# Two decoder layers on one core: the latent keys' token factors spread over the partitions by two transfers through DRAM

## The chip, the cores and the metric

The kernel runs on one core of a Trainium2 chip. The metric is the device time of one execution in microseconds (us); before the change its median over three runs is 1880.4 us (1880.3 to 1882.12). PE is the matrix engine, DVE the vector engine, ACT the scalar engine, POOL the GpSimd engine, and SP issues most of the loads. Each engine works through its own list of instructions in the order in which the list was written at build time, and waits where an instruction needs something that another engine or a transfer has not finished.

## The reference, cut to what matters

Two layers of a decoder trunk over 512 tokens and 1024 channels. In each layer a branch of multi-head latent attention makes keys and values from a normalised low-rank vector `c_kv` of 256 channels per token:

```
kv = (rmsnorm(c_kv, norm_kv) @ w_ukv).reshape(bsz, seq, MLA_HEADS, QK_NOPE + V_DIM)
k_nope, v = kv[..., :QK_NOPE], kv[..., QK_NOPE:]
```

with `rmsnorm(x, g) = x * rsqrt(mean(x*x) + EPS) * g`. The factor `rsqrt(...)` is one number per token. Four heads have 128 key and 128 value channels each. Around this branch stand the combined input projection, a convolution branch, sparse attention, a merge of the branches, cross attention and a SwiGLU block.

## The kernel before

Products are made three times over with high and low parts of each operand (lines 86 to 88: high by high, high by low, low by high), and `hilo` (lines 93 and 94, or 96 and 97 with a scale) makes these parts: ACT writes the high part, DVE the low part. Weights come by SP into `raw`, become `wh` and `wl`, and are used once.

The token factors of the latent attention are made in `mix`, once in each layer. PE sums the squares of the latents per token into one bank (`means`, line 1210), so that the tokens lie on the partitions: column t holds tokens 128 t to 128 t + 127. DVE adds the epsilon (line 1213) and POOL takes the power -1/2 (line 1214). Of the tile `rst`, columns 0 to 3 then hold the four query factors and columns 4 to 7 the four key factors. The latents are kept without their factor, and it is put in later:

- `values` has the tokens on the partitions, so the factor is a scale per partition (`rst[:, 4 + t]`, lines 96 and 97).
- `keys(h)` has the key channels on the partitions and the 512 tokens along the row, so it needs the factors as a row of 512 numbers, the same on all 128 partitions. This is the tile `rk`; line 846 multiplies the product in PSUM by it (`kf`), and `hilo` splits the result.

`scales` makes `rk`. DVE multiplies the identity by each of the four columns (line 820, tile `dg`, four diagonal blocks of 128), PE multiplies a tile of ones by `dg` (line 833), which puts each token's factor on every partition, and ACT copies the bank to `rk` (line 835). `scales` also splits the weights of keys and values (`weights`).

The code of `mix` runs several strands in turn: `pump` hands out steps of `filler`, which are the input projection's products for the sparse attention, so that PE has work between the dependent steps of the latent attention. A scheduler then puts every engine's instructions in an order at build time. The banks of PSUM are few: tags `mm` (3), `pv` (1), `s` (2) and `t` (2). `idle` hands out `s`, `t`, `s`, `t`, `pv` in turn for queries, keys, `turned` (transposes of the rotated queries, drained at lines 409 and 410) and values. A product on PE waits until DVE and ACT have read the bank that it takes over.

POOL issues background transfers of its own: sums of weight blocks from DRAM to DRAM (`up`, `down`, `mixed`, line 481) which a much later stage reads. Each of them waits for a certain product on PE (`tick`), and POOL stands still until then. The powers and a few small fills stand in the same list.

Of the kernel before, what the change touches and what calls it, by code (L numbers as in the profile page):

```python
# [10 lines left out]
F32 = mybir.dt.float32  # L11
# [3 lines left out]
OP = mybir.AluOpType  # L15
# [6 lines left out]
NT = T // 128  # L22
# [30 lines left out]
def kernel(ctx, tc, x, mem, positions, rel_bias, norm_mix, norm_xattn, norm_mem, norm_ffn, norm_final,  # L53
# [5 lines left out]
    nc = tc.nc  # L59
# [6 lines left out]
    dr = ctx.enter_context(tc.tile_pool(name="dr", bufs=1, space=DRAM))  # L66
# [7 lines left out]
    def new(tag, shape=(128, 512), dt=F32, name=None):  # L74
        return (odd if tag in ODD else sb).tile(list(shape), dt, name=name or tag, tag=tag, bufs=BUFS[tag])

    def bank(tag, name=None):
        return ps.tile([128, 512], F32, name=name or f"ps_{tag}", tag=tag, bufs=PBUFS[tag])
# [11 lines left out]
    def hilo(hi, lo, src, scale=None):  # L90

        if scale is None:
            nc.scalar.copy(hi, src)  # L93
            nc.vector.tensor_tensor(lo, src, f(hi), op=OP.subtract)  # L94
        else:
            nc.scalar.activation(hi, src, AF.Copy, scale=scale)
            nc.vector.scalar_tensor_tensor(lo, src, scale, f(hi), op0=OP.mult, op1=OP.subtract)
# [68 lines left out]
    ident = cst.tile([128, 128], F32, name="ident")  # L166
    ones = cst.tile([128, 128], F32, name="ones")
# [318 lines left out]
    def mix(l, x_src, g_mix, x_now, more_x, spill_x, turns, memory):  # L486
# [136 lines left out]
        for i, wu in enumerate(fm_blocks(W, [Z_CQ, Z_CQ + 128, Z_CQ + 256, Z_CKV, Z_CKV + 128], KD)):  # L623
            p = bank("mm")
# [190 lines left out]

        def scales():
            nc.vector.tensor_scalar(rst[:, 8:12], rst[:, 0:4], -(128 + 64) ** -0.5, None, op0=OP.mult)
            dg = new("P", name="dg")
            for t in range(NT):
                nc.vector.tensor_scalar(dg[:, t * 128:(t + 1) * 128], ident, rst[:, 4 + t:5 + t], None, op0=OP.mult)  # L820
            rv = kv_raw.rearrange("p (k h c) -> p k h c", k=2, h=4)

            def weights(c0):
                w = new("wh", (128, 1024), F32R), new("wl", (128, 1024), F32R)
                for k in range(2):
                    hilo(w[0][:, k * 512:(k + 1) * 512].rearrange("p (h c) -> p h c", h=4),
                         w[1][:, k * 512:(k + 1) * 512].rearrange("p (h c) -> p h c", h=4), rv[:, k, :, c0:c0 + 128])
                wk.append(w)

            weights(0)  # L830
            yield
            p = bank(next(idle))
            nc.tensor.matmul(p, ones, dg, start=True, stop=True)
            rk = new("gm", name="rk")
            nc.scalar.copy(rk, p)
            weights(128)
            yield rk

# [362 lines left out]
        idle = cycle(("s", "t", "s", "t", "pv"))  # L1201
# [6 lines left out]
        for i, q in enumerate(sq):  # L1208
            for t in range(NT):
                nc.tensor.matmul(means[:, i * 4 + t:i * 4 + t + 1], q[:, t * 128:(t + 1) * 128], ones[:, 0:1],  # L1210
                                 start=True, stop=True)
        rst = new("rst", (128, 16))
        nc.vector.tensor_scalar(rst[:, 8:16], means[:, 0:8], EPS, None, op0=OP.add)
        nc.gpsimd.tensor_tensor(rst[:, 0:8], rst[:, 8:16], mhalf, op=OP.pow)

        scale = scales()
        qrot = []
        for t in range(NT):
            p = bank(next(idle))
# [8 lines left out]
            rk = next(scale) if t % 2 else None  # L1228
# [263 lines left out]
    for l in range(L):  # L1492
# [75 lines left out]
        for h, wu in enumerate(fm_blocks(w_xkv[l], [128 * h for h in range(4)], KD)):  # L1568
            p = bank("mm")
# [177 lines left out]
        for i, wu in enumerate(fm_blocks(w_gate_up[l], cols, KD)):  # L1747
            m = i % 2
            p = bank("mm")
# [189 lines left out]
```

## Time and profile before

| | |
|---|---|
| median of three runs | 1880.4 us |
| profiled execution, its own time | 1880.6 us |
| span of the profiled execution | 1878.9 us |
| clock granted to PE | 0.999 of full |
| DVE busy | 1554.9 us (83%) |
| ACT busy | 1067.9 us (57%) |
| POOL busy | 317.8 us (17%) |

The profiled execution lies within the three runs. The two places that make `rk` lie at about 85 to 89 us (first layer) and 1016 to 1019 us (second layer) from the start of the span. In the rows of the timeline the first number is the start, the second how long the instruction or the run of instructions took; the bracket at a row's end gives the idle time of that engine just ahead of it and what ended it.

### The profile page before, as it was taken

What the parts mean: (1) busy time and instruction counts of PE and PEld (TensorE: products, weight loads), DVE (VectorE), ACT (ScalarE), POOL (GpSimd) and SP (SyncE); (2) the same over time, 40 slices, a digit from 0 to 9 for tenths busy, and PEclk for the clock granted to TensorE, in tenths of its full rate; (3) what the DMA queues carried; (4) which work ended last, traced back from release to release, by engine and by line L of the source; (5) the groups of instructions that cost most, each with busy time, mean ns of one, the idle gap of its engine ahead of it and who ended that gap; (6) DMA issues with size and microseconds to landing.
All of it is one profiled execution on the core that took longest, in us unless ns stands there. A gap on an engine that the chain in (4) does not pass through costs nothing.

```text
span 1878.9 us, 29709 instructions
## 1 busy us (share of the span) xinstructions
PE 1863.0 (99%) x10940; PEld 1634.2 (87%) x10940; DVE 1554.9 (83%) x2842; ACT 1067.9 (57%) x1992; POOL 317.8 (17%) x501
## 2 busy tenths in 40 slices
PE   9999999999999999999999999999999999999998
PEld 8888888888887999998888888888888889999986
DVE  6999998765966899898869999986659678899886
ACT  5367557764555545456544755686636455445564
POOL 1211112112121212200022111121121122212000
PEclk9999999999999999999999999999999999999999
DMA  6665765568774778876666666655786747877764
GB/s 188 160 164 158 186 151 142 132 165 201 230 213 129 197 193 219 224 218 200 180 188 166 167 176 169 150 120 137 172 212 206 222 139 194 215 192 215 229 191 162
DMA packets 229901, 341.60 MB, mean 182 GB/s; under 512 B 17600, under 2 KB 157139, under 8 KB 229756
## 3 DMA queue, kind: packets, MB, share of 16 engines
q1 hardware_dynamic: 188460, 222.68, 37.4%
q0 software_dynamic: 39360, 112.22, 28.5%
q10 hardware_dynamic: 1936, 4.81, 0.7%
q8 instruction: 86, 1.41, 0.3%
q14 instruction: 59, 0.48, 0.1%
HBM read 330.20 MB, written 114.32 MB: 237 GB/s over the span
## 4 chain that ended last, share of the span: by engine, by line
PE 86%; DVE 5%; issue 5%; POOL 1%; ACT 1%; DMA 1%; SPq 0%; POOLq 0%; DVEq 0%; ACTq 0%
PE ps_mm L86 15%; PE ps_mm L88 14%; PE ps_mm L87 14%; PE ps_s L86 3%; PE ps_s L88 2%; PE ps_s L87 2%; PE ps_t L88 2%; PE ps_t L87 2%; PE ps_t L86 2%; PE ps_t L1130 2%; PE ps_mm L1440 1%; PE ps_mm L1441 1%; PE ps_mm L1439 1%; PE ps_pv L86 1%; PE ps_s L1439 1%
## 5 line engine op out<-in xcount | busy, mean ns | idle before, releaser
L93 ACT CAST wh<-raw 128x1024 fp32r<-128x1024 f32 (+4 forms) x429 | 434.9, 1016 | 473.6 <-PE ps_mm L87 110.8
L94 DVE TENSOR_TENSOR wl<-raw,wh 128x1024 fp32r<-128x1024 f32 (+4 forms) x429 | 503.1, 1177 | 173.3 <-ACT wh L93 169.6
L86 PE MATMUL ps_mm<-hTh,wh 128*128 128x512 f32 (+1 forms) x1152 | 415.1, 361 | 0.0
L87 PE MATMUL ps_mm<-hTl,wh 128*128 128x512 f32 (+1 forms) x1152 | 411.2, 357 | 0.0
L88 PE MATMUL ps_mm<-hTh,wl 128*128 128x512 f32 (+1 forms) x1152 | 410.5, 357 | 0.5 <-DVE wl L94 0.5
L88 PEld LDWEIGHTS ps_mm<-hTh,wl 128*128 128x128 f32 x1152 | 217.8, 189 | 32.8 <-DVE wl L94 1.3
L86 PEld LDWEIGHTS ps_mm<-hTh,wh 128*128 128x128 f32 x1152 | 217.9, 189 | 28.4 <-issue 1.3
L87 PEld LDWEIGHTS ps_mm<-hTl,wh 128*128 128x128 f32 x1152 | 218.0, 189 | 26.2 <-issue 0.7
L602 DVE SCALAR_TENSOR_TENSOR ca<-u,vT,ca 128x512 f32<-128x512 f32 x240 | 177.7, 747 | 2.8
L481 POOL DMA_DIRECT2D up<-in_w_gate_up_dram x128 | 84.7, 662 | 459.8 <-PE ps_mm L88 343.8
L481 POOL DMA_DIRECT2D down<-in_w_down_dram x132 | 87.8, 674 | 287.3 <-PE ps_mm L88 134.4
L93 ACT CAST PTh<-ps_t 128x512 fp32r<-128x512 f32 (+4 forms) x136 | 70.2, 516 | 50.6 <-PE ps_t L1130 43.8
L1093 ACT ACTIVATE P<-P,ss 128x512 f32<-128x512 f32 (+3 forms) x128 | 71.5, 559 | 48.2 <-DVE ss L1090 47.2
L86 PE MATMUL ps_s<-rh,wh 128*128 128x256 f32 x320 | 90.6, 283 | 0.0
L87 PE MATMUL ps_s<-rl,wh 128*128 128x256 f32 x320 | 90.6, 283 | 0.0
L88 PE MATMUL ps_s<-rh,wl 128*128 128x256 f32 x320 | 90.6, 283 | 0.0
L94 DVE TENSOR_TENSOR PTl<-ps_t,PTh 128x512 fp32r<-128x512 f32 (+2 forms) x120 | 71.7, 599 | 10.2 <-ACT PTh L93 9.1
L1101 ACT ACTIVATE P<-P,sr 128x512 f32<-128x512 f32 (+3 forms) x128 | 63.2, 555 | 13.7 <-DVE sr L1099 13.6
L481 POOL DMA_DIRECT2D down<-down x44 | 35.5, 807 | 189.4 <-DMA down<-down 79.1
L200 POOL TENSOR_TENSOR rs<-rs,mhalf 128x1 f32<-128x1 f32 x25 | 24.1, 964 | 229.9 <-DVE rs L197 229.8
L86 PEld LDWEIGHTS ps_s<-rh,wh 128*128 128x128 f32 x320 | 61.4, 192 | 0.0
L87 PEld LDWEIGHTS ps_s<-rl,wh 128*128 128x128 f32 x320 | 61.4, 192 | 0.0
(598 smaller groups left out, 4803.8 us busy)
## 6 DMA issues: line engine op xcount, KB each, us to landing
up<-in_w_gate_up_dram POOLq DMA_DIRECT2D x128, 320.0 KB, 4.4
down<-in_w_down_dram POOLq DMA_DIRECT2D x132, 256.0 KB, 5.1
raw<-in_w_in_dram SPq DMA_DIRECT2D x30, 1024.0 KB
raw<-in_w_gate_up_dram SPq DMA_DIRECT2D x60, 512.0 KB
raw<-up SPq DMA_DIRECT2D x40, 512.0 KB
raw<-down SPq DMA_DIRECT2D x40, 512.0 KB
raw<-in_w_in_dram SPq DMA_DIRECT2D x30, 512.0 KB
raw<-in_w_down_dram SPq DMA_DIRECT2D x30, 512.0 KB
```

What stands on the lines that cost most here:

```text
L86: nc.tensor.matmul(o, lh, rh, start=start, stop=False)
L87: nc.tensor.matmul(o, lh, rl, start=False, stop=False)
L88: tick(nc.tensor.matmul(o, ll, rh, start=False, stop=stop))
L93: nc.scalar.copy(hi, src)
L94: nc.vector.tensor_tensor(lo, src, f(hi), op=OP.subtract)
L200: latest["power"] = nc.gpsimd.tensor_tensor(r[:, 1:2], r[:, 0:1], mhalf[:, 0:1], op=OP.pow)
L481: d = nc.gpsimd.dma_start(dst, src, accum_op=op) if op else nc.gpsimd.dma_start(dst, src)
L602: nc.vector.scalar_tensor_tensor(c, u[:, j:j + T], cw[:, m, j:j + 1], c, op0=OP.mult, op1=OP.add)
L1093: nc.scalar.activation(p[:, c], p[:, c], AF.Exp, bias=s[:, k:k + 1], scale=-1.0, accum_out=s[:, 4 + k:5 + k])
L1101: nc.scalar.activation(P[k], P[k], AF.Copy, scale=r[:, k:k + 1])
L1130: nc.tensor.transpose(tp[:, w:w + 128], P[k][:, j * 128:(j + 1) * 128], ident)
L1439: nc.tensor.matmul(accs[t], xh, u[0][:, k, :], start=j == 0 and not goes_on, stop=False, **kw)
```

## The change

The diagonal tile, the product with ones and the copy out of PSUM go. In their place stand two transfers that POOL issues: one writes columns 4 to 7 of `rst`, 128 x 4 numbers, into a small DRAM tile `spread` in the order of the tokens, and one reads these 512 numbers back to all 128 partitions of `rk`. The call that took a bank from `idle` stays without the bank, so the turns of the banks don't shift.

```diff
         def scales():
             nc.vector.tensor_scalar(rst[:, 8:12], rst[:, 0:4], -(128 + 64) ** -0.5, None, op0=OP.mult)
-            dg = new("P", name="dg")
-            for t in range(NT):
-                nc.vector.tensor_scalar(dg[:, t * 128:(t + 1) * 128], ident, rst[:, 4 + t:5 + t], None, op0=OP.mult)
+            spread = dr.tile([NT, 128], F32, name=f"spread{l}")
+            rk = new("gm", name="rk")
+            nc.gpsimd.dma_start(spread.rearrange("t p -> p t"), rst[:, 4:8])
+            nc.gpsimd.dma_start(rk, bass.AP(tensor=spread.tensor, offset=spread.offset, ap=[[0, 128], [1, 512]]))
             rv = kv_raw.rearrange("p (k h c) -> p k h c", k=2, h=4)
...
             weights(0)
             yield
-            p = bank(next(idle))
-            nc.tensor.matmul(p, ones, dg, start=True, stop=True)
-            rk = new("gm", name="rk")
-            nc.scalar.copy(rk, p)
+            next(idle)
             weights(128)
             yield rk
```

The lines of the new kernel are one higher from 821 to 831 and two lower from 834 on (846 becomes 844).

The scheduler writes some instructions near the place in another order. Three places follow. The first is POOL's list in the first layer, from the power (line 1214 before, 1212 now) on. Before:

```order
L1214 TENSOR_TENSOR rst<-rst,mhalf 128x8
L481 DMA up_2_149<-in_w_gate_up_dram 64x1280
L481 DMA up_0_148<-in_w_gate_up_dram 64x1280
L481 DMA up_2_149<-in_w_gate_up_dram 64x1280
L481 DMA up_0_148<-in_w_gate_up_dram 64x1280
L593 MEMSET u 128x30
```

Now:

```order
L1212 TENSOR_TENSOR rst<-rst,mhalf 128x8
L820 DMA spread_956<-rst 128x4x1
L481 DMA up_2_149<-in_w_gate_up_dram 64x1280
L821 DMA rk<-spread_956 128x512
L481 DMA up_0_148<-in_w_gate_up_dram 64x1280
L481 DMA up_2_149<-in_w_gate_up_dram 64x1280
L481 DMA up_0_148<-in_w_gate_up_dram 64x1280
L593 MEMSET u 128x30
```

The write stands right behind the power, one background sum behind it, and then the read, which waits for the write to have landed. The second layer has the same order.

The second place is DVE's list in the second layer, from the split of the second head's `kf` to the product of the third head with `rk` (`xf` and `xt` are inputs of the sparse attention's compression, `wl` the low part of weights that PE waits for). Before:

```order
L94 TENSOR_TENSOR op_10923<-kf_10924,op_10922 128x512
L664 TENSOR_TENSOR xf_10945<-ps_mm_10791,vT_10175 64x496
L410 SCALAR_TENSOR_TENSOR op_10933<-ps_t_10928,op_10933 64x512
L94 TENSOR_TENSOR xt_10942<-xf_10945,xt_10942 128x8x31 x2
L664 TENSOR_TENSOR xf_10945<-ps_mm_10791,vT_10175 64x496
L410 SCALAR_TENSOR_TENSOR op_10936<-ps_t_10928,op_10936 64x512
L664 TENSOR_TENSOR xf_10945<-ps_mm_10791,vT_10175 64x496
L94 TENSOR_TENSOR wl_10962<-raw_10958,wh_10961 128x1024
L94 TENSOR_TENSOR xt_10942<-xf_10945,xt_10942 128x8x31 x2
L846 TENSOR_TENSOR kf_10979<-ps_pv_10969,rk_10866 128x512
```

Now:

```order
L94 TENSOR_TENSOR op_10913<-kf_10914,op_10912 128x512
L410 SCALAR_TENSOR_TENSOR op_10923<-ps_t_10918,op_10923 64x512
L94 TENSOR_TENSOR xt_10932<-xf_10935,xt_10932 128x8x31 x2
L664 TENSOR_TENSOR xf_10935<-ps_mm_10786,vT_10170 64x496 x2
L410 SCALAR_TENSOR_TENSOR op_10926<-ps_t_10918,op_10926 64x512
L94 TENSOR_TENSOR xt_10932<-xf_10935,xt_10932 128x8x31 x2
L94 TENSOR_TENSOR wl_10952<-raw_10948,wh_10951 128x1024
L844 TENSOR_TENSOR kf_10969<-ps_pv_10959,rk_10811 128x512
```

One `xf` moved ahead of the first of these rows, and the last pair of `xt` moved from behind `wl` to ahead of it. In the first layer it is the other way round: there a pair of `xt` moved from ahead of `wl` to behind it. On PE, two products of `values` that stood behind the product with this `wl` now stand ahead of it in the second layer; in the first layer one product of the input projection moved from ahead of it to behind it.

The third place is ACT's list in the second layer, from the split of the fourth head's `kf` to the first softmax of the latent attention (`P`; the scale of the finished row is line 888 before, 886 now). Before:

```order
L93 CAST op_10996<-kf_10998 128x512
L93 CAST wh_11198<-raw_10792 128x1024
L96 ACTIVATE op_11010<-ps_t_11002,rst_10771 128x512
L96 ACTIVATE op_11021<-ps_s_11014,rst_10771 128x512
L886 ACT_TABLE_LOAD
L886 ACTIVATE P_11054,s1_11055<-P_11054,s1_11055 128x512
L96 ACTIVATE op_11032<-ps_t_11025,rst_10771 128x512
L93 CAST w1_11208<-raw_11210 128x512
L96 ACTIVATE op_11044<-ps_pv_11036,rst_10771 128x512
L888 ACTIVATE P_11054<-P_11054,s1_11055 128x512
```

Now:

```order
L93 CAST op_10986<-kf_10988 128x512
L93 CAST wh_11188<-raw_10787 128x1024
L96 ACTIVATE op_11000<-ps_t_10992,rst_10766 128x512
L96 ACTIVATE op_11011<-ps_s_11004,rst_10766 128x512
L96 ACTIVATE op_11022<-ps_t_11015,rst_10766 128x512
L96 ACTIVATE op_11034<-ps_pv_11026,rst_10766 128x512
L93 CAST w1_11198<-raw_11200 128x512
L93 CAST w1_11199<-raw_11200 128x512
L93 CAST wh_11306<-raw_11303 128x1024
L884 ACT_TABLE_LOAD
L884 ACTIVATE P_11044,s1_11045<-P_11044,s1_11045 128x512
```

Two splits of `values`, two of `w1` and the split of the next weights `wh` moved ahead of the table load and the first exponential.

## The prediction

> **What bounds the kernel now.** I read the page's busy times and its chain first, then the two stretches where `rk` is made. Each row is busy time and share of the span; the second is the chain that ended last.
>
> ```profile
> PE 1863.0 (99%) x10940; PEld 1634.2 (87%) x10940; DVE 1554.9 (83%) x2842; ACT 1067.9 (57%) x1992; POOL 317.8 (17%) x501
> PE 86%; DVE 5%; issue 5%; POOL 1%; ACT 1%; DMA 1%; SPq 0%; POOLq 0%; DVEq 0%; ACTq 0%
> ```
>
> PE is hardly ever idle. So work taken from PE is worth its length, a wait that PE takes on costs its length, and work off PE counts only where PE waits for it. The timeline of PE has one such wait in each of the two stretches, and both are for DVE:
>
> ```profile
> 102.56 0.47 PE L86 MATMUL ps_t<-wh,op 128*128 128x512 f32 x1 [0.25 <-DVE op L410]
> 104.38 0.50 PE L88 MATMUL ps_mm<-hTh,wl 128*128 128x512 f32 x1
> 1033.72 0.50 PE L88 MATMUL ps_mm<-hTh,wl 128*128 128x512 f32 x1 [0.46 <-DVE wl L94]
> ```
>
> In the second layer the chain of waits shows where this wait begins (start, time on the chain, what):
>
> ```profile
> 1021.92 0.70 DVE kf L846
> ...
> 1032.44 1.24 DVE wl L94
> 1033.72 0.50 PE ps_mm L88
> ```
>
> From the first head's `kf`, the first user of `rk`, the chain runs through DVE (with short turns by ACT) to `wl` and from there to PE. DVE has next to no slack in these 12 us, so a late `rk` goes on to PE in full.
>
> **What goes.** The product with ones, on the chain of each layer, and beside it the diagonal tile on DVE and the copy on ACT:
>
> ```profile
> 87.42 0.86 PE ps_pv L833 x2
> 1017.52 0.86 PE ps_pv L833 x2
> 85.07 0.28 DVE L820 TENSOR_SCALAR dg<-ident,rst 128x128 f32<-128x128 f32 x1
> 85.27 0.42 DVE L573 TENSOR_TENSOR qr<-qr,rt 128x256 f32<-128x256 f32 x1
> 85.60 0.67 DVE L820 TENSOR_SCALAR dg<-ident,rst 128x128 f32<-128x128 f32 x3
> 86.19 1.28 DVE L94 TENSOR_TENSOR wl<-raw,wh 128x512 fp32r<-128x512 f32 x2
> 88.51 0.58 ACT L835 COPY rk<-ps_pv 128x512 f32<-128x512 f32 x1
> 92.55 0.62 ACT L93 CAST op<-kf 128x512 fp32r<-128x512 f32 x1 [3.46 <-DVE kf L846]
> ```
>
> PE gains 0.86 us per layer. DVE gains 0.20 + 0.59 = 0.79 us (from each start to the next). ACT's copy was followed by 3.46 us of idling; it counts nothing. Before, `kf` waited for PE and not for `rk`:
>
> ```profile
> 91.82 0.69 DVE L846 TENSOR_TENSOR kf<-ps_s,rk 128x512 f32<-128x512 f32 x1 [0.35 <-PE ps_s L88]
> 1021.92 0.69 DVE L846 TENSOR_TENSOR kf<-ps_s,rk 128x512 f32<-128x512 f32 x1 [0.45 <-PE ps_s L88]
> ```
>
> With PE 0.86 us ahead, and DVE ahead by enough, `kf` wants `rk` at 90.96 and 1021.06 us.
>
> **What comes: the path of the two transfers.** They start behind the power on POOL:
>
> ```profile
> 82.09 2.10 POOL L1214 TENSOR_TENSOR rst<-rst,mhalf 128x8 f32<-128x8 f32 x1 [3.08 <-DVE rst L1213]
> 1013.96 1.67 POOL L1214 TENSOR_TENSOR rst<-rst,mhalf 128x8 f32<-128x8 f32 x1 [0.22 <-DVE rst L1213]
> ```
>
> The powers end at 84.19 and 1015.63 us. If the write and the read take p us together, `rk` is late by x0 = 84.19 + p - 90.96 = p - 6.77 in the first layer and x1 = 1015.63 + p - 1021.06 = p - 5.43 in the second. Neither transfer is in the trace. The nearest rows are transfers that POOL issues: the tile `xd` (first row, 256 KB from SBUF to DRAM) and the tile `md` (second, the same size and direction) as smallest, median and largest time to landing, and the DRAM-to-DRAM sums with their median:
>
> ```profile
> DMA to landing us min/median/max: 2.2/2.5/4.1
> DMA to landing us min/median/max: 4.3/6.1/6.5
> up<-in_w_gate_up_dram POOLq DMA_DIRECT2D x128, 320.0 KB, 4.4
> DMA to landing us min/median/max: 3.0/4.4/7.8
> ```
>
> (The last is `up` with its ends.) The write is 512 pieces of 4 bytes. SP's one load of that shape, the positions, took longer to issue than a plain small load:
>
> ```profile
> 19.75 0.96 SPq L335 DMA_DIRECT2D pos_i<-in_positions_dram  x1
> 21.58 0.37 SPq L363 DMA_DIRECT2D rb<-in_rel_bias_dram  x1
> ```
>
> Write: between 2.2 and 6.5 us; I take 3.1, the median of `xd` plus the 0.6 that the small pieces cost in issue. Read, 256 KB from DRAM: between 3.0 and 7.8 us (`up`); I take its median, 4.4, since it too is read from DRAM on POOL's queue. So p = 7.5, between 5.2 and 14.3; x0 = 0.73 and x1 = 2.07 us.
>
> The Trainium skill bears on the write in two ways. In "DMA: Bandwidth & Descriptors", section "Anatomy of one DMA — SWDGE (gpsimd) path", a transfer issued from GpSimd costs 2.0 us plus its bytes over 436 GB/s; as an estimate that is 2.0 + 2.6 = 4.6 us for both, and the sum below would be that of the first rival. It fits the median of `xd` (2.5) and not those of `md` (6.1) and `up` (4.4). The same page's "Rules for kernel authors" says that a non-contiguous last dimension becomes one descriptor per element, which speaks against this write; the row of `pos_i` agrees in kind, and it would make the second rival likelier.
>
> **The sum.** First layer: the next place that DVE sets is PE's product with `wl` at 104.38.
>
> ```profile
> 103.11 1.22 DVE L94 TENSOR_TENSOR wl<-raw,wh 128x1024 fp32r<-128x1024 f32 x1
> 102.45 0.75 DVE L94 TENSOR_TENSOR xt<-xf,xt 128x248 fp32r<-128x248 f32 x2
> ```
>
> In the new order this pair of `xt` (0.66, start to start) stands behind `wl`, and one product (0.23) behind PE's. So `wl` ends at 104.33 - 0.86 - 0.66 + x0 = 102.81 + x0 and the product starts 0.05 later, against 104.38 - 0.23 = 104.15 for the same state of PE's work: x0 - 1.29. PE alone (its stands of about 0.5 ahead of this product gone too) would arrive at about 102.8, so no more is to be had.
>
> Second layer: the pair of `xt` stands ahead of `wl`, whose end is 1033.68 - 0.86 + 0.66 + x1 = 1033.48 + x1, the product 0.05 later; by then two products of `values` are done that stood behind it, 0.45 from the first row to the second:
>
> ```profile
> 1035.44 0.39 PE L87 MATMUL ps_t<-wl,op 128*128 128x512 f32 x1
> 1035.89 0.39 PE L86 MATMUL ps_pv<-wh,op 128*128 128x512 f32 x1
> ```
>
> Against 1033.72: x1 - 0.19 - 0.45 = x1 - 0.64.
>
> Together x0 + x1 - 1.93 = 0.73 + 2.07 - 1.93 = **+0.9 us**. On the profiled execution's 1880.6 (span 1878.9, the rest lies around it, and the median is 0.2 lower) that is 1881.4.
>
> Edits that I cost at nothing. ACT's new order in the second layer puts a weight split, which waits for a load, ahead of the first softmax:
>
> ```profile
> 1041.91 0.99 SPq L102 DMA_DIRECT2D raw<-in_w_in_dram  x2
> 1046.34 1.05 ACT L93 CAST wh<-raw 128x1024 fp32r<-128x1024 f32 x1
> 1039.86 1.28 ACT L886 ACT_TABLE_LOAD   x1
> 1043.54 0.71 ACT L888 ACTIVATE P<-P,s 128x512 f32<-128x512 f32 x1
> 1048.68 0.27 PE L897 MATMUL ps_t<-ident,P 128*128 128x128 f32 x1
> ```
>
> The load goes out about 2.0 us sooner, since the `wl` that frees its buffer now stands ahead of 2.0 us of DVE's work; it landed in at most 4.43 us, so `wh` starts near 1044.3, and with the split, the table and three activations `P` is done near 1048.6 instead of 1044.25. PE wants it at 1048.68, 0.3 later by its own shift. It fits by 0.3 us; a load slower by 1 us would cost 0.7. On POOL, the sums and a fill of `u` queue behind the read, which waits some 3 us for the write. The sums are first read at 615.8 us, and `u` has 14 us:
>
> ```profile
> L1790 SPq DMA_DIRECT2D raw<-up x40: 366/367/1349, 615.8 to 1739.8; - x40
> 1038.24 0.40 POOL L593 MEMSET u<- 128x30 f32 x1
> 1052.91 0.67 DVE L596 SCALAR_TENSOR_TENSOR u<-th,ps_mm 128x512 f32<-128x512 f32 x1
> ```
>
> Were that cover gone, it would cost those 3 us. On DVE, the convolution's steps, the splits, the drains at line 410 and `wl` queue behind `kf`; PE waits for the last two.
>
> **Rivals.**
> - *The transfers are hidden.* With p below 5.4 neither layer waits and the whole -1.93 stays: 1878.7. For it: the median and the minimum of `xd`, and an almost idle DMA ahead of the first layer's write. Against: the read stands behind a background sum on the same queue. Even this is a gain of only 0.1%.
> - *The transfers are late (slower).* If the write goes like `md` (6.1) and the read takes 5.7, as the broadcast of a gain at the start did at most,
>
> ```profile
> 1.26 0.45 ACTq L190 DMA_DIRECT2D gB<-in_norm_mix_dram  x1
> 6.98 1.42 DVE L283 SCALAR_TENSOR_TENSOR hn<-x,rs,gB 128x512 f32<-128x512 f32 x2 [1.03 <-DMA gB<-in_norm_mix_dram]
> ```
>
>   then p = 11.8, x0 + x1 = 11.4 and the time 1890.1. It is over 0.2% slower from x0 + x1 = 5.7, that is from p = 8.95 on. For it: the small pieces, and the sums that share the queue. Against: that broadcast was twice as large, amid a burst of loads.
> - *The new order costs by itself.* The thin 0.3 us at the first softmax turns into a wait of 1 to 2 us: 1882.4 to 1883.4 with the forecast's p.
>
> **How the numbers follow.** About 0.2%, 3.8 us, is what a measurement of this kernel can tell from no change. Forecast (p between 5.4 and 8.95): 0.48. Hidden: 0.20. Late: 0.22. The order alone: 0.10, within 0.2% but for a small part. Faster by over 0.2% needs more than the whole removed work; I leave 0.05, taken from the hidden case. Slower by over 0.2%: 0.24. Within: 0.71. The forecast's own range is 1878.7 to 1884.3; the full one reaches down to the hidden case and up to the late one, 1878.0 to 1890.0. The worst rows (p = 14.3) would give 1895; that is the part left out.
>
> **What would show it.** Right: no L833, L820 of before or L835; PE 1.7 us less busy; an idle time of DVE ahead of the first `kf`, ended by the transfer into `rk`, larger in the second layer by about 1.3 us; PE's waits at L410 or `wl` in both stretches longer by about as much as that idle time grew. Wrong: `kf` still waiting for PE alone (hidden), idle times of 4 us and more (late), or PE waiting for `P` at the first transposes of the second layer. The prediction is wrong in kind if POOL's write takes several us to issue, or if PE's waits elsewhere in the span change by over 1 us.

## The result and the profile after

The changed kernel takes 1907.0 us (median of four runs, 1904.6 to 1907.8) against 1880.35 us for the kernel before in the same comparison: a ratio of 1.0139, with a 95% interval of 1.0127 to 1.0151. The forecast was 1881.4 us with a range up to 1890. The profiled execution has a span of 1905.0 us, 26.1 more than before. From its page, the busy time of the engines and the chain that ended last:

```profile
PE 1865.9 (98%) x10936; PEld 1637.4 (86%) x10936; DVE 1553.6 (82%) x2834; ACT 1067.3 (56%) x1990; POOL 320.7 (17%) x505
PE 77%; DVE 9%; issue 6%; DMA 3%; ACT 3%; POOL 2%; SPq 0%; POOLq 0%; ACTq 0%; DVEq 0%
```

PE has four instructions fewer and is still 2.9 us busier, and its idle time has grown from 15.9 us (1878.9 - 1863.0) to 39.1 us. PE's waits (what, for whom, total, times, longest) say where:

```profile
PE ps_mm L86 <- ACT wh L93: 22.8, 2, 12.7
PE ps_t L88 <- DVE wl L94: 1.9, 3, 0.8
...
PE ps_t L895 <- ACT P L886: 0.8, 1, 0.8
```

The same view of before has no wait for `wh` at this line. Now PE has it once in each layer, for 10.1 and 12.7 us. The timeline has the two transfers and the `kf` that wants `rk` (the first three rows are the first layer, the others the second):

```profile
84.77 0.84 POOL L820 DMA_DIRECT2D spread<-rst  x1 [0.30 <-POOL rst L1212]
...
94.58 0.58 POOL L821 DMA_DIRECT2D rk<-spread  x1 [8.11 <-DMA spread<-rst]
...
101.92 0.69 DVE L844 TENSOR_TENSOR kf<-ps_s,rk 128x512 f32<-128x512 f32 x1 [10.99 <-DMA rk<-spread]
...
1025.90 0.83 POOL L820 DMA_DIRECT2D spread<-rst  x1 [0.31 <-POOL rst L1212]
...
1036.09 0.57 POOL L821 DMA_DIRECT2D rk<-spread  x1 [8.83 <-DMA spread<-rst]
...
1044.32 0.69 DVE L844 TENSOR_TENSOR kf<-ps_s,rk 128x512 f32<-128x512 f32 x1 [13.66 <-DMA rk<-spread]
```

The read can go out 9.8 us (94.58 - 84.77) and 10.2 us after the write, and `kf` starts another 7.3 and 8.2 us later. From the write's issue to `kf` that is 17.2 and 18.4 us. The prediction's p runs from the end of the power, 0.3 us before that issue (see the brackets), to the landing of the read; by its count p is 17.4 and 18.6 us, where 7.5 was forecast. DVE stands idle for 11.0 and 13.7 us ahead of `kf`. The chain of the first layer (start, time, what) goes from there to PE by a way that the prediction did not name:

```profile
94.58 7.25 DMA rk<-spread
...
101.92 0.70 DVE kf L844
...
102.65 0.63 ACT op L93
...
104.74 0.60 ACT op L409
...
105.36 1.05 ACT wh L93
...
106.45 0.80 PE ps_mm L86
107.25 0.43 PE ps_mm L87
```

ACT works in the order of its list. The split of `kf` stands ahead of a weight split (`wh`, line 93), so all of PE's filler work stops with it. The last row shows one thing more: a product takes 0.43 us from start to start, where it took 0.23. Windows of 2 us (length, busy times with instruction counts of PE, PE's weight loads, DVE, ACT and POOL, then granted PE clock, busy share of the DMA engines, GB/s) show why, and what the DMA engines did meanwhile. The first row's share, above 1, stands as the view prints it and is not used here:

```profile
86.00:88.00 2.00, 2.00 (x15) 1.83 (x14) 2.00 (x7) 0.53 (x2) 0.48 (x1) 1.00 2.37 32
...
94.00:96.00 2.00, 2.00 (x13) 1.67 (x11) 0.00 (x0) 0.00 (x0) 1.42 (x3) 1.00 0.32 15
...
98.00:100.00 2.00, 0.00 (x0) 0.00 (x0) 0.00 (x0) 0.00 (x0) 0.00 (x0) 0.82 1.13 263
100.00:102.00 2.00, 0.00 (x0) 0.00 (x0) 0.08 (x1) 0.00 (x0) 0.00 (x0) 0.50 0.96 317
...
106.00:108.00 2.00, 1.55 (x4) 1.27 (x5) 1.94 (x4) 1.51 (x3) 0.00 (x0) 0.50 0.54 105
```

While the write is under way, from 86 to 96 us, the DMA engines move 3 to 32 GB/s in each window, though a background sum of 320 KB is queued behind it and, from 90.3 us on, a load of weights; from 96 to 104 us, with the write landed, they move 201 to 317. And the clock granted to PE falls to half during the pause and is still there when PE resumes. So four things stood to be told apart: the time of the write, the time of the read, what the write does to other transfers, and what PE's pause adds.

### The profile page after: what moved, and what is told of

The parts are those of the page before. It is cut to its first block, busy times and chain, and to the rows that moved or that the text cites. A ratio compares the mean times of both kernels' runs of the same rounds, so it can differ in the third digit from the quotient of the medians.

```text
span 1905.0 us, 29702 instructions
## 1 busy us (share of the span) xinstructions
PE 1865.9 (98%) x10936; PEld 1637.4 (86%) x10936; DVE 1553.6 (82%) x2834; ACT 1067.3 (56%) x1990; POOL 320.7 (17%) x505
## 3 DMA queue, kind: packets, MB, share of 16 engines
q0 software_dynamic: 39584, 112.75, 29.1%
q10 hardware_dynamic: 1936, 4.81, 0.7%
## 4 chain that ended last, share of the span: by engine, by line
PE 77%; DVE 9%; issue 6%; DMA 3%; ACT 3%; POOL 2%; SPq 0%; POOLq 0%; ACTq 0%; DVEq 0%
PE ps_mm L86 13%; PE ps_mm L87 13%; PE ps_mm L88 13%; PE ps_s L86 2%; PE ps_s L88 2%; PE ps_s L87 2%; DVE wl L94 2%; PE ps_t L88 2%; PE ps_t L86 2%; PE ps_t L87 2%; PE ps_t L1128 2%; DVE ca L602 1%; PE ps_mm L1438 1%; PE ps_mm L1439 1%; PE ps_mm L1437 1%
## 5 line engine op out<-in xcount | busy, mean ns | idle before, releaser
L86 PE MATMUL ps_mm<-hTh,wh 128*128 128x512 f32 (+1 forms) x1152 | 415.0, 361 | 22.8 <-ACT wh L93 22.8
```

The costliest lines, as they stand in the source:

```text
L86: nc.tensor.matmul(o, lh, rh, start=start, stop=False)
```

## The experiments

Thirteen kernels ran, each compared with the kernel before on the same chip. Ratios are to the kernel before, with 95% intervals.

| run | median us | ratio |
|---|---|---|
| changed kernel | 1907.0 | 1.0139 (1.0127 to 1.0151) |
| e1_16b | 1887.3 | 1.0038 (1.0023 to 1.0053) |
| e10_8b | 1891.8 | 1.0059 (1.0044 to 1.0074) |
| e2_quiet | 1908.9 | 1.0155 (1.0140 to 1.0170) |
| e6_actq | 1904.6 | 1.0130 (1.0111 to 1.0148) |
| e3_nowait | 1898.2 | 1.0101 (1.0084 to 1.0118) |
| e5_before_write | 1894.7 | 1.0073 (1.0058 to 1.0088) |
| e12_late | 1907.5 | 1.0140 (1.0125 to 1.0155) |
| e4_read_only | 1881.2 | 1.0005 (0.9995 to 1.0014) |
| e9_none | 1881.5 | 1.0005 (0.9995 to 1.0014) |
| e7_rows | 1884.2 | 1.0021 (1.0012 to 1.0030) |
| e8_early | 1878.3 | 0.9991 (0.9982 to 1.0000) |
| e11_busy | 1925.4 | 1.0241 (1.0224 to 1.0258) |
| e13_busy | 1911.2 | 1.0164 (1.0147 to 1.0181) |

### What the write costs: the number of its pieces

e1_16b writes four numbers of a partition as one piece:

```diff
-            spread = dr.tile([NT, 128], F32, name=f"spread{l}")
+            spread = dr.tile([128, NT], F32, name=f"spread{l}")
-            nc.gpsimd.dma_start(spread.rearrange("t p -> p t"), rst[:, 4:8])
+            nc.gpsimd.dma_start(spread, rst[:, 4:8])
```

> The changed kernel with one edit: spread is laid out as 128 x 4, so each partition writes its four numbers as one piece of 16 bytes (128 pieces, not 512 of 4 bytes). The 512 numbers come back in another order, so each key is multiplied by another token's factor. Theory 1 (the write's time is its number of pieces): the write lands in 3 to 4 us instead of 9 to 10, kf waits some 6 us less in each layer, PE's two long waits shrink by as much: 1891 to 1895 us. Rival, theory 2 (the background sums on the same queue set the time): the write still takes 8 us or more, 1903 to 1907. Rival, theory 3 (the read sets it): the write was not the larger part, the read stays at 7 to 8 us, and the gain is under 6 us in all.

e10_8b lies between, with two pieces of 8 bytes for each partition:

```diff
+            spread = dr.tile([2, 128, 2], F32, name=f"spread{l}")
...
+            nc.gpsimd.dma_start(spread.rearrange("a p b -> p a b"), rst[:, 4:8].rearrange("p (a b) -> p a b", a=2))
```

> The changed kernel with the write in 256 pieces of 8 bytes, half as many as in the changed kernel and twice as many as in e1_16b (the factors come back in another order, so each key takes another token's factor). Theory 1, the price goes by the number of pieces: the write lands in 4.5 to 5.5 us, 1891 to 1897 us. Rival (pieces under 16 bytes are slow whatever their number): 8 us or more, 1902 to 1907. Second rival (the price is in 4-byte pieces alone): about 2 us, 1886 to 1889.

From the timeline of e1_16b, first layer:

```profile
84.53 0.63 POOL L820 DMA_DIRECT2D spread<-rst  x1 [0.30 <-POOL rst L1212]
...
86.59 0.58 POOL L821 DMA_DIRECT2D rk<-spread  x1 [0.58 <-DMA spread<-rst]
...
92.69 0.69 DVE L844 TENSOR_TENSOR kf<-ps_s,rk 128x512 f32<-128x512 f32 x1 [1.86 <-DMA rk<-spread]
```

And of e10_8b:

```profile
84.49 0.80 POOL L820 DMA_DIRECT2D spread<-rst  x1 [0.30 <-POOL rst L1212]
...
89.08 0.60 POOL L821 DMA_DIRECT2D rk<-spread  x1 [2.91 <-DMA spread<-rst]
```

The same 2 KB take 2.1, 4.6 and 9.8 us from the write's issue to the read's, with 128, 256 and 512 pieces. The two steps are 2.5 us for 128 pieces more and 5.2 us for 256 more: 0.020 us for each added piece, both times. That price does not start at zero: in e8_early below, four pieces of 512 bytes take 1.9 us (84.91 - 83.05), about as long as 128 pieces of 16 bytes. So a write of 2 KB cost some 2 us here even with few pieces, and the price of the pieces showed only beyond 128. The number of pieces and their size changed together in these runs and were not told apart further. Theory 1 holds in this form: e10_8b came within its range, and e1_16b 3.7 us below its own. The Trainium skill, in "DMA: Bandwidth & Descriptors", section "Rules for kernel authors", says that a last dimension that is not contiguous becomes one descriptor per element. These runs agree in kind, and give a price for this shape.

e2_quiet holds the background sums back around the place:

```diff
         idle = cycle(("s", "t", "s", "t", "pv"))
+        paced["rate"] = 0.0
...
             keys(h)
+            if h == 0:
+                paced["rate"] = 0.22
```

> The changed kernel with the background sums held back from the queries until the first head's keys are done, and issued a little faster from there on, so no sum is under way between the write and the read. Theory 1 (pieces): the write still takes about 9 us, the read falls to 3 to 5 us, since no sum stands ahead of it; 1897 to 1902 us. Theory 2 (sums on the queue): write near 3, read near 4 us, kf hardly waits, 1879 to 1884. Theory 3 (the broadcast read is slow by itself): read 7 to 8 us as before, 1903 to 1908.

Its timeline, first layer:

```profile
84.33 0.84 POOL L820 DMA_DIRECT2D spread<-rst  x1 [0.31 <-POOL rst L1213]
...
94.75 0.57 POOL L821 DMA_DIRECT2D rk<-spread  x1 [9.58 <-DMA spread<-rst]
```

The write takes 10.4 us with no sum near it, so the sums do not make it slow; theory 2 falls. The read took 5.6 and 6.4 us to landing, not 3 to 5, and the time, 1908.9 us, lies 6.9 us above the range of theory 1 and just above that of theory 3. The sums that were held back changed the engines' lists far beyond the place, and new waits appeared (2.8 us for `w` in the compression at line 714, 3.1 us for `P`), so the time of this run is no test.

e6_actq lets ACT issue the write on its own queue:

```diff
-            nc.gpsimd.dma_start(spread.rearrange("t p -> p t"), rst[:, 4:8])
+            nc.scalar.dma_start(spread.rearrange("t p -> p t"), rst[:, 4:8])
```

> The changed kernel with the write of 512 pieces issued by ACT on its own queue instead of by POOL; the read stays on POOL. Theory 1 (some 0.02 us for each piece, as 128, 256 and 512 pieces gave 2.1, 4.6 and 9.8 us from issue to the read's issue): still 8 to 11 us, SP's load held up as before, 1902 to 1910 us. Rival (POOL's queue makes the pieces slow): 2 to 4 us, 1884 to 1890.

From its timeline, first layer:

```profile
84.31 0.40 ACTq L820 DMA_DIRECT2D spread<-rst  x1
...
93.72 0.60 POOL L821 DMA_DIRECT2D rk<-spread  x1 [8.63 <-DMA spread<-rst]
```

That is 9.4 us again, and 12.6 in the second layer. So the price belongs to the pieces, not to POOL or its queue; why the second write took 3 us longer is open. This run also lets the pieces be counted. The page's packets of ACT's queue go from 1936 in the kernel before to 2992, 528 more for each of the two writes, which is 512 and a few. For POOL's queue the page has the same number of packets with 512, 256, 128 and 4 pieces (39584), so there the number of pieces is taken from the access pattern.

### The late load: what the write does to others

e3_nowait keeps both transfers but takes the user of `rk` away:

```diff
-            nc.vector.tensor_tensor(kf, p, rk, op=OP.mult)
+            nc.vector.tensor_tensor(kf, p, mask, op=OP.max)
```

> The changed kernel with both transfers in place, but kf does not read rk: it takes the elementwise maximum with the mask tile, which is long there (the key factor is left out). Every engine's list has the same order as in the changed kernel. Theory of the wait (the whole loss is kf waiting for rk, and what PE's pause brings with it): nobody waits, the removed work shows, 1878 to 1880 us. Rival (the transfers cost by themselves, by taking POOL's list, the DMA engines or the loads' time): 1884 us or more, with PE waiting elsewhere.

This was the surprise of the study: nobody waits for `rk`, and the kernel is still 17.8 us slower than before. PE's waits and the chain of the first layer:

```profile
PE ps_mm L86 <- ACT wh L93: 14.4, 2, 8.2
```

```profile
90.09 13.18 DMA raw<-in_w_in_dram
103.37 1.05 ACT wh L93
104.47 0.79 PE ps_mm L86
```

SP's load of the next projection weights goes out at 90.09 us, when the write's pieces and then the broadcast are on the DMA engines, and takes 13.2 us. In e9_none below, without the transfers, the chain has the same kind of load of the second layer at 5.36 us. So the wait theory, which had the whole loss in `kf`, was wrong as it stood.

e5_before_write adds the write alone to the kernel before, with the product with ones in place and no user of `spread`:

```diff
+            spread = dr.tile([NT, 128], F32, name=f"spread{l}")
+            nc.gpsimd.dma_start(spread.rearrange("t p -> p t"), rst[:, 4:8])
             dg = new("P", name="dg")
```

> The kernel before, with its product with ones kept, plus the write of 512 pieces into spread behind the power on POOL; nothing reads spread. Theory 4 (the pieces hold up the DMA engines, and with them SP's load of the next weights): the write lands after 9 to 10 us, the load that goes out near 90 us lands at 99 to 102 instead of about 95, PE waits 4 to 8 us for wh in each layer, 1888 to 1897 us. Rival (the write costs only by making rk late): 1880 to 1882 us.

Its waits of PE, and the load on the chain of the first layer:

```profile
PE ps_mm L86 <- ACT wh L93: 12.6, 2, 6.4
```

```profile
90.97 11.28 DMA raw<-in_w_in_dram
```

A write of 2 KB that nobody reads costs 14.1 us of kernel time (1894.7 against 1880.6), through a load of 11.3 us in each layer. PE waits 6.2 and 6.4 us for it, and is 3.3 us busier than in the kernel before (1866.3 against 1863.0) for the same products. That confirms theory 4. Which part of the engines' work the load waits behind (their order within a queue or across queues) was not tried.

### The late factors alone

e12_late has no write and no pieces. It makes the read of e4_read_only late by small powers on POOL:

```diff
...
+            for _ in range(12):
+                late = nc.gpsimd.tensor_tensor(rst[:, 12:16], rst[:, 0:4], mhalf[:, 0:4], op=OP.pow)
+            d = nc.gpsimd.dma_start(rk, rows_bcast(w_in[l], 512))
...
```

> The read of e4_read_only (no write), made late by 12 small powers on POOL ahead of it, so that rk lands near 102 and 1044 us as in the changed kernel, with no pieces on the DMA engines. Theory 5 (the late rk alone stops PE, since ACT's wh split stands behind the split of kf): DVE idles 10 to 14 us ahead of the first kf, PE waits for wh as in the changed kernel, 1900 to 1907 us; then the load's delay and rk's run side by side. Rival (the two add up, and the load's delay, which e3_nowait shows alone, is the larger): 1887 to 1892 us.

From its timeline of DVE, and its waits of PE:

```profile
106.71 0.69 DVE L846 TENSOR_TENSOR kf<-ps_s,rk 128x512 f32<-128x512 f32 x1 [14.60 <-DMA rk<-in_w_in_dram]
...
1051.69 1.29 DVE L846 TENSOR_TENSOR kf<-ps_s,rk 128x512 f32<-128x512 f32 x2 [14.72 <-DMA rk<-in_w_in_dram]
```

```profile
PE ps_mm L86 <- ACT wh L93: 28.9, 2, 14.9
```

The powers took longer than meant, so `rk` is late by 29.3 us in all instead of 24.7, and PE waits 28.9 for it: nearly one for one. The kernel is 26.9 us slower than before, a little more than the range allowed, as the lateness is. In proportion to a lateness of 24.7 that would be 22.7 of the changed kernel's 26.6, as an estimate from these two runs. Theory 5 holds, and its rival, that the two add up, falls. So the load's delay (14 to 18 us alone) and the factors' lateness run side by side in the changed kernel, and the later of the two ends PE's pause. In its chain above that is `kf`; the load of e3_nowait lets `wh` start at 103.37, and `kf` only at 105.36.

### The read, and the rest of the change, alone

e4_read_only drops the write and broadcasts 512 numbers from a weight instead, at the same place (a dependency ties it behind the power):

```diff
...
-            nc.gpsimd.dma_start(spread.rearrange("t p -> p t"), rst[:, 4:8])
-            nc.gpsimd.dma_start(rk, bass.AP(tensor=spread.tensor, offset=spread.offset, ap=[[0, 128], [1, 512]]))
+            d = nc.gpsimd.dma_start(rk, rows_bcast(w_in[l], 512))
...
```

> The changed kernel without the write: rk is read, broadcast in the same way, from the first 512 numbers of the input projection's weight, right behind the power on POOL (key factors are replaced by these numbers). Theory 3 (the broadcast read is slow by itself): 7 to 8 us to landing, kf waits 1 to 3 us in each layer, 1880 to 1886 us. Rival (the read was slow only because it stood behind a sum that the write held up): 3 to 5 us, kf waits for PE alone, 1878 to 1880.

What the trace answers for the tile `rk` (smallest, median, largest):

```profile
DMA to landing us min/median/max: 3.8/3.8/3.9
```

The broadcast by itself takes 3.8 us, near the 4.4 of the prediction, so theory 3 falls. It reads another tensor here, but e8_early, which reads `spread`, has 3.8 and 4.2 us. So the 7.3 and 8.2 us of the changed kernel belong to what runs beside the read. That this is the sum and the load which the write had held up fits e2_quiet, where the load runs without a sum and the read takes 5.6 and 6.4 us; no run takes the two apart. Yet the time, 1881.2 us, is not the 1878 to 1880 of a hidden read. e9_none takes both transfers out:

```diff
...
-            nc.gpsimd.dma_start(spread.rearrange("t p -> p t"), rst[:, 4:8])
-            nc.gpsimd.dma_start(rk, bass.AP(tensor=spread.tensor, offset=spread.offset, ap=[[0, 128], [1, 512]]))
...
-            nc.vector.tensor_tensor(kf, p, rk, op=OP.mult)
+            nc.vector.tensor_tensor(kf, p, mask, op=OP.max)
```

> The changed kernel without either transfer; kf takes the maximum with the mask (the key factor is left out). It is the removed work and the new order alone. By the prediction's sum for rk in time, 1878.7 us. Rival (the new order costs by itself, as the waits of e4_read_only for the first softmax's P, 1.6 us, and for wh, 1.2 us, suggest): 1880 to 1881.5 us, with PE's wait for P at the transposes of the second layer still there.

Its page, its waits of PE, the load on its chain, and ACT's timeline in the second layer:

```profile
PE 1860.4 (99%) x10936; PEld 1633.0 (87%) x10936; DVE 1553.7 (83%) x2834; ACT 1066.8 (57%) x1990; POOL 317.8 (17%) x501
```

```profile
PE ps_t L891 <- ACT P L882: 1.1, 1, 1.1
...
PE ps_mm L86 <- ACT wh L93: 1.0, 1, 1.0
```

```profile
1019.76 5.36 DMA raw<-in_w_in_dram
...
1025.22 1.05 ACT wh L93
```

```profile
1044.12 1.05 ACT L93 CAST wh<-raw 128x1024 fp32r<-128x1024 f32 x1 [1.96 <-DMA raw<-in_w_in_dram]
1045.19 1.28 ACT L880 ACT_TABLE_LOAD   x1
```

PE is 2.6 us less busy than before, and the kernel is no faster (1.0005), since two new waits take most of the gain back; the span of the profiled execution is 0.4 us shorter than before. That execution, at 1880.3 us, lies 1.2 us below the median of this kernel, and the profile does not show where those 1.2 us go. PE, now earlier, stands 1.0 us for a weight split whose load goes out only when a split on DVE has freed its buffer, and 1.1 us for the first softmax, which in the new order of ACT stands behind a split that waits for its own load. The first of the two loads (5.36 us) is the one that the write held up, and PE waits for it even undisturbed, so it had no slack to take a delay. The second wait is the prediction's third rival. Its `wh` started at 1044.12, forecast 1044.3, but that is luck in part: the load went out at 1038.74 instead of 1039.9 and took 5.28 us instead of 4.43, and the two errors cancel.

### Repairs

e7_rows writes four pieces of 512 bytes, from factors that PE has transposed and ACT has copied out of the bank:

```diff
+            p = bank(next(idle))
+            nc.tensor.transpose(p[0:NT, 0:128], rst[:, 4:8], ident)
+            row = new("P", name="row")[0:NT, 0:128]
+            nc.scalar.copy(row, p[0:NT, 0:128])
-            nc.gpsimd.dma_start(spread.rearrange("t p -> p t"), rst[:, 4:8])
+            nc.gpsimd.dma_start(spread, row)
...
-            next(idle)
             weights(128)
```

> The factors are first transposed on PE (128 x 4 to 4 x 128, into a bank) and copied to SBUF by ACT, so that the write has 4 pieces of 512 bytes; the read is unchanged. By theory 1 the write lands within 2 to 2.5 us and holds nothing up; the transpose, the copy and their waits add about 2 us ahead of it, the read takes 5.5 to 6 behind one sum, kf waits 2 to 4 us in each layer: 1885 to 1890 us. Rival (any write and dependent read through DRAM costs 8 us or more here): 1892 or more.

From its timeline of DVE, a row of each layer:

```profile
92.77 0.69 DVE L847 TENSOR_TENSOR kf<-ps_s,rk 128x512 f32<-128x512 f32 x1 [1.23 <-DMA rk<-spread]
...
1027.29 1.29 DVE L847 TENSOR_TENSOR kf<-ps_s,rk 128x512 f32<-128x512 f32 x2 [2.22 <-DMA rk<-spread]
```

`kf` waits 1.2 and 2.2 us, and the loss is 0.2%; the time lies 0.8 us below the range that was expected. e8_early makes the factors earlier as well, by moving the means and the power ahead of the second pair of query heads:

```diff
         queries(0)
-        queries(2)
...
         nc.gpsimd.tensor_tensor(rst[:, 0:8], rst[:, 8:16], mhalf, op=OP.pow)
+        queries(2)
+        spread = dr.tile([NT, 128], F32, name=f"spread{l}")
+        rk = new("gm", name="rk")
...
+        nc.gpsimd.dma_start(spread, row)
```

> e7_rows with the means and the power moved ahead of the second pair of query heads, 18 products or 4.1 us earlier on PE; transpose, write and read are issued where the means stood. If lateness of rk and the pieces are the whole loss, kf no longer waits for rk or for less than 1 us, and the time is that of e9_none, 1879.5 to 1882 us. Rival (the read takes longer beside the loads that follow the queries): kf still waits 2 us or more, 1884 or more.

From its timeline, the write, the read and the first `kf` of the first layer:

```profile
83.05 0.55 POOL L1215 DMA_DIRECT2D spread<-row  x1 [2.23 <-ACT row L1214]
...
84.91 0.58 POOL L1216 DMA_DIRECT2D rk<-spread  x1 [0.49 <-DMA spread<-row]
...
91.42 0.68 DVE L839 TENSOR_TENSOR kf<-ps_s,rk 128x512 f32<-128x512 f32 x1
```

No idle time stands ahead of `kf` any more. The time is 1878.3 us, 2.1 us below the kernel before and 1.2 below the range that was expected; PE no longer waits for `P` here, for a reason that the runs leave open. The interval, 0.9982 to 1.0000, just touches no change, so a real gain is likely but small.

### The clock

PE is 5.5 us busier in the changed kernel than in e9_none (1865.9 against 1860.4) with the same number of instructions. e11_busy was to keep PE working through the pause with 40 spare products in each layer:

```diff
...
+            if h == 3:
+                held_bank = bank(next(idle))
+                for _ in range(40):
+                    nc.tensor.matmul(held_bank, cqT[0][0][:, 0:128], cqT[0][0], start=True, stop=True)
...
```

> The changed kernel with 40 spare products (9.2 us at 0.23 us each, into the bank that the fourth head's keys take next) put on PE in each layer ahead of the products that wait for wh, so that PE works through most of its pause. They add work only where PE stood idle. If the granted clock falls because PE pauses, it stays at 1.00, the 5.5 us that PE is busier in the changed kernel than in e9_none go, and the time is 1901 to 1904 us. Rival (the clock falls for another reason, or its fall is hidden by waits): 1906 to 1909 us.

It tells nothing of the clock: the scheduler put the spare products behind the product that waits for `wh`, so they only lengthened the kernel by their 18 us. e13_busy has 52, one head earlier (`if h == 2`) and ahead of that head's `pump(2)`:

> As e11_busy, but with the spare products (52 in each layer, 12 us at 0.23 us each, into the bank of the third head's keys) ahead of the product that waits for wh. ACT's wh stands one key split and two drains later than in the changed kernel, so PE's pause ends some 3 us later in each layer and the time itself is no test. If the pause brings the clock down, the granted clock stays at 1.00 in both stretches and PE is busy for e9_none's 1860.4 and 104 x 0.23 = 23.9 us, 1884.3 in all; the time is 1903 to 1911 us. Rival (the clock falls for another reason): PEclk 0.50 again near 100 and 1042 us and PE busy 1888 us or more.

Windows of e13_busy in the first layer, with the columns as above:

```profile
100.00:104.00 4.00, 4.00 (x20) 3.30 (x19) 1.53 (x3) 0.83 (x2) 0.26 (x1) 1.00 0.84 287
...
108.00:110.00 2.00, 0.19 (x1) 0.00 (x0) 1.31 (x3) 1.17 (x2) 0.00 (x0) 1.00 0.00 0
110.00:112.00 2.00, 1.48 (x4) 1.24 (x5) 1.94 (x4) 0.95 (x3) 0.00 (x0) 0.72 0.00 0
112.00:114.00 2.00, 2.00 (x6) 1.51 (x6) 1.96 (x5) 0.22 (x1) 0.79 (x1) 0.50 0.44 36
```

With PE at work the clock is 1.00 at 100 to 104 us, where it was 0.50 in the changed kernel. But a pause was left over behind the spare products (2.3 us in this layer, 4.9 in the other), and the clock fell after it: the fall moved with the pause. PE was busy for 1888.4 us, not for the 1884.3 of an undisturbed clock, so the saving itself was not shown. The Trainium skill, in "TensorE: Matmul & The Clock Gate", "Part 1: The HAM clock gate (the "warmup" mystery)", puts the fall to half rate after an idle window of about 3.4 us. The windows here agree with that only roughly. In the changed kernel PE ran dry at 96.4 us, and a mean of 0.82 from 98 to 100 us, between 1.00 and 0.50, puts the fall at 99.3, 2.9 us later; in the second layer the same reckoning gives 5.2 us. And the pause of 2.3 us in e13_busy was shorter than 3.4 us: the mean of 0.72 from 110 to 112 us puts the fall at 110.9, when PE had been back at work for 0.4 us. Shorter pauses left the clock at 1.00, as one of 1.4 us in e1_16b and one of 1.9 us in e7_rows.

## Why the prediction was wrong

- **The size of p, the term on which the sum rested.** It was 7.5 us with bounds of 5.2 and 14.3, and measured 17.4 and 18.6 by the same count. Of the two terms in it the write was the larger miss, 9.8 and 10.2 us to the read's issue where 3.1 was taken; the read took 7.3 and 8.1 us to landing where 4.4 was taken. The write was priced by the tile `xd`, 256 KB in long pieces, and its 512 pieces at 0.6 us because `pos_i` took 0.6 longer *to issue*. The issue was indeed short (0.84 us); the cost of the pieces came after it, 0.020 us for each beyond 128. No row of the trace of before had a transfer of that shape with its landing, and the bounds came from rows that were alike in bytes but not in pieces. The bound that deserved distrust was the upper one.
- **The formula was better than its input.** With the lateness as measured, x0 + x1 = 11.0 + 13.7 = 24.7, the sum x0 + x1 - 1.93 gives +22.7 against a span 26.1 longer, and for e12_late 29.3 - 1.93 = +27.4 against 27.7. The closeness of the second is luck in part: the 1.93 did not show as a gain (e9_none), and nothing in the sum stands for the products that ran at half clock after the pause. The statement that a late `rk` goes on to PE almost in full was right: PE waits 22.8 us for 24.7 of lateness, and 28.9 for 29.3. The layer difference was forecast as 1.3 us and was 2.7.
- **The way to PE was wrong.** It was to go through DVE's drains (line 410) and `wl`. It went through ACT's list, where the split of `kf` stands ahead of `wh`, and stopped the filler work too. PE's waits for `wl` at line 88 grew by only 0.8 us: the one into `ps_t` from 0.6 to 1.9, while the 0.5 into `ps_mm` went.
- **No term for the neighbours.** "An almost idle DMA" was read as a reason for a fast write, and nothing was charged for what the write does to the loads behind it. e5_before_write shows that as 14.1 us by itself. In the changed kernel it hides for the most part behind the late factors, so it adds little there. But with no one waiting for the factors (e3_nowait) 17.8 us of loss were left, and with late factors and no write (e12_late, where the factors came later still) 26.9, so mending only the one or the other would not have been enough.
- **No term for the clock.** Two pauses of 10 us and more left PE 5.5 us busier than in e9_none for the same products. The 26.5 us between the two spans are thus 21.0 of idle time (39.1 against 18.1) and 5.5 of busy time. That half clock is behind most of the 5.5 us is an estimate from the timeline: after the two pauses 21 products took 9.6 us together, and at 0.23 us each they would have taken 4.8. No run had such pauses without the fall. The size goes by when the clock comes back and not by the length of the pause: in e12_late, with longer pauses, 19 products took 8.7 us, and PE was 3.2 us busier than in e9_none.
- **The gain of 1.93 us** did not appear either (e9_none, 1.0005). The thin place at the first softmax was named as a rival with a chance of 0.10, and it happened. Another 1.0 us was lost to a weight load for which PE came too early, which was not foreseen.
- **The rivals.** The late one had the right sign and mechanism, a late `rk` behind a slow write, with p = 11.8 instead of 17.4 and 18.6, and got 0.22; but 1907.0 us lies well beyond its 1890.1 too. The page of the Trainium skill that spoke against a last dimension in pieces was cited beside the forecast and given too little weight. The size formula of the same page, by which both transfers were 4.6 us and the first rival's sum would hold, came out far too low for this shape.
- **The tests of the prediction** did most of their work: idle times of 4 us and more ahead of `kf`, ended by the transfer, were its sign of the late case, and they were there. Its signs of being wrong in kind did not show: POOL's write was short to issue, and outside the two stretches no wait of PE changed by 1 us. The wait that grew lay in the two stretches, but for `wh` at line 93, which no test had named.

## What to carry to other kernels

Price a small transfer in pieces by the number of its pieces as well as by its bytes, and if no row of the trace has that shape, let the upper bound say so. Ask of each new transfer not only who waits for it but what is queued on the same DMA engines behind it; here 2 KB that nobody read cost 0.7%. And when a wait is put on one engine, look down the lists of all engines that take its result in order: the first instruction behind it that feeds PE decides, whether or not it has to do with the change.

## What the hardware did that was not expected

- Writes of 2 KB to DRAM took 2.1, 4.6 and 9.8 us with 128, 256 and 512 pieces of 16, 8 and 4 bytes, which is 0.020 us for each piece beyond 128. Four pieces of 512 bytes took 1.9 us in e8_early, and landed after 2.8 and 3.5 us in e7_rows. From ACT's queue 512 pieces took 9.4 and 12.6 us, from POOL's 9.8 and 10.2.
- While such a write ran, a load of weights from SP's queue took 11.3 us (e5_before_write) instead of 5.4, and in the changed kernel's first layer the DMA engines moved 3 to 32 GB/s.
- After pauses of 2.3 to 14.9 us PE's granted clock fell to 0.50, 2 to 5 us after PE had run dry, and products took 0.43 us instead of 0.23 for some 3 to 6 us of PE's work. After pauses of 1.4 and 1.9 us it did not fall.
